# Two more gates in a pair and one written order on all engines, in the gate stage of a hybrid decoder step

## The chip, the core and the metric

The kernel runs on one core of a Trainium2 chip. The metric is the device time of one execution in microseconds (us). TensorE is the matrix engine (PE in the profile, its weight loads PEld), VectorE is DVE, ScalarE is ACT, GpSimd is POOL, and SyncE is SP, which here only issues transfers.

## What is computed

One layer of a decoder, for 512 prompt tokens and 8 sample tokens (one each), together N = 520 columns, D_MODEL = 2048. Two token mixers read the same normed input `h`. The first is a matrix memory and doesn't matter here. The second is forgetting attention with 8 heads of 128. A sigmoid gate for each channel merges them:

```python
mq, mk, mv, mo, mi, mf, fq, fk, fv, ff, ga, gb = jnp.split(h @ w_in + b_in, SPLIT_POINTS, axis=-1)
...
y_f = fox_fn(q_f, k_f, v_f, lf_f)
merged = jax.nn.sigmoid(ga) * (y_m @ w_proj_a) + jax.nn.sigmoid(gb) * (y_f @ w_proj_b)
x = x + g1 * (merged @ w_out)
```

For the prompt, `fox_prompt` is causal attention with cumulated log forget values added to the scores. For the samples, `fox_sample` takes 256 past keys and values of each sample from two pages of 128 rows in a cache, through a page table. A feed-forward part follows. All is float32; the kernel writes each operand as a high and a low part in a format that TensorE takes at full rate and sums three products (high by high, high by low, low by high).

## The kernel before

**Gates.** The pre-activations of `gb` are 16 chunks of 128 channels, called gates. Each is a product of 2048 rows of weights by `h`. There are two ways to compute one. `dense` (line 197) takes a gate by itself: 16 blocks by three products by two column halves are 96 matmuls of 260 columns. Its weights come in two halves of 1024 columns, each loaded raw (`wraw`, line 158), cast on ScalarE to `wh` and subtracted on VectorE to `wl` (`wtwo`, lines 164 to 169). A `GatePair` computes two gates at once by a scheme of seven products instead of eight on sums of the operands (`Pair`, `run_pairs`): 7 by 8 by 3 are 168 matmuls of 260 columns, plus sums of weights on VectorE. Pairs read the forms `hX` of `h`, and they stand in the stage before, between 8 pairs for queries and keys and 4 for values. `NB2 = 4` gates of `gb` are in pairs; the twelve others go through `dense` in the loop at line 1826, the gate stage.

**The second mixer behind the gates.** The attention is cut into small functions that are run between the matmuls of the gate stage. `dense` calls `step()` after every six matmuls, which takes the next entry of the list `bg`; the loop has 12 by 16 = 192 such steps. A table `plan`, filled by `put(step, function)` from line 1767 on, says what each step runs. Head hh starts at step b = 1 + 22 hh: it is loaded 20 steps earlier (`f_load`, five transfers on SP), normed (`f_norm`), split in high and low parts (`f_split` on ScalarE, `f_split_low` on VectorE at b + 4), its scores follow at b + 8 to b + 12 (`f_scores` on TensorE, `f_max` on VectorE with an exponential on ScalarE, `f_scale`), the turns of the weights at b + 19 on (`f_turn`, `f_turn_low`), and the products with the values at b + 26 to b + 29 (`f_attend`, whose last one also copies the result `yf`).

**Pages.** For the samples, 16 page pairs of keys (8 samples by two halves of the heads) are fetched by `s_load` (one row of q on SP, two gathers of 256 KB on POOL) at step 6 + 7i, and `s_scores` (step 18 + 7i) multiplies and reduces both pages on VectorE. Then `s_bias`, `s_turn`, `s_max`, `s_scale`, `s_weights` and `s_places` make the softmax from step 126 on, 32 gathers of values (`s_gather`) go out four for each of eight `s_attend` (tile `sO`, every five steps from 137), whose results are turned (`s_heads`, tile `sOT`) and added (`s_add`).

**What sets the order.** The kernel is written for a framework that places instructions on each engine's queue by their priority and by when it believes their operands ready, and gives out buffers from pools (33 tiles of tag `s`, nine `p`, seven `raw`, three each of `wh` and `wl`, four PSUM banks `mm`, two accumulators `acc`). `Ordered` (line 53) pins an instruction behind the one traced before it on its engine. In the pairs T, V and S (TensorE, VectorE, ScalarE) are pinned; in the gate stage only those of VectorE that are written through `MV`. Weight loads, casts and subtractions of `dense` are under a high priority, so they are placed as early as tiles allow. After the gates, sixteen products with `w_pb` follow (tile `pb`, from line 2001 on), which read `yf`.

Of the kernel before, what the change touches and what calls it, by code (L numbers as in the profile page):

```python
# [18 lines left out]
P = 128  # L19
# [3 lines left out]
NS = 8  # L23
# [40 lines left out]
def tile_hybrid_step(ctx: ExitStack, tc: tile.TileContext, I, O):  # L64
    nc = tc.nc
    S, V, G, T = nc.scalar, nc.vector, nc.gpsimd, nc.tensor
# [1194 lines left out]
    NB2 = 4  # L1261
# [133 lines left out]
    def root_load():  # L1395
        root["v"] = v = pt("rv")
        nc.sync.dma_start(v[:, :65], dss.rearrange("e h n -> (e h n)").rearrange("(p c) -> p c", p=P))
# [12 lines left out]
    def rows_load():  # L1410
        root["x"], root["r"] = pt("xr"), pt("rb")
        for e in range(2):
            o = slice(e * 64, e * 64 + 64)
            nc.sync.dma_start(root["x"][:, o].rearrange("p (h n) -> p h n", h=FH),
                              dqk[e, :, :, SEQ:N].rearrange("h p n -> p h n"))
            nc.sync.dma_start(root["r"][:, o].rearrange("p (h n) -> p h n", h=FH),
                              drr[e, :, SEQ:N].partition_broadcast(P))
# [12 lines left out]
    def s_rows(e):  # L1430
# [4 lines left out]
        nc.sync.dma_start(dqf[e].rearrange("b (h d) -> (b h) d", h=4), qrow[:32, :P])  # L1435

    def s_load(i):
# [3 lines left out]
        nc.sync.dma_start(qb[:, :512], dqf[e, b].partition_broadcast(P))  # L1441
# [4 lines left out]

    MV = Ordered(tc, nc.vector)
# [10 lines left out]
    def f_load(H):  # L1458
        H.q, H.k, H.rq, H.rk, H.v = (st("fi") for _ in range(5))
        for t, src in ((H.q, dqk[0, H.i]), (H.rq, drr[0, H.i].partition_broadcast(P)), (H.k, dqk[1, H.i]),  # L1460
                       (H.rk, drr[1, H.i].partition_broadcast(P)), (H.v, dv[H.i])):
            nc.sync.dma_start(t[:, :N], src)

    def f_norm(H):
        for t, w, r in ((H.q, qwc, H.rq), (H.k, nkw, H.rk)):
            MV.scalar_tensor_tensor(t[:, :N], t[:, :N], w, r[:, :N], op0=ALU.mult, op1=ALU.mult)
# [80 lines left out]
    T, V, S = nc.tensor, nc.vector, nc.scalar  # L1547
# [9 lines left out]
    psb = mm_ps("sbias")  # L1557
    o0 = psb[:, 0:64].rearrange("p (b h) -> p b h", b=NS)
    o1 = psb[:, 64:128].rearrange("p (b h) -> p b h", b=NS)
    T.matmul(o0, ups[:, :P], lg4[:, 0], start=True, stop=False)  # L1560
    T.matmul(o0, ones, lg4[:, 1], start=False, stop=False)
    T.matmul(o0, ones[:FH, :], lfd, start=False, stop=True)
    T.matmul(o1, ups[:, :P], lg4[:, 1], start=True, stop=False)
    T.matmul(o1, ones[:FH, :], lfd, start=False, stop=True)
    sbias = mconst([P, NPG, NS, FH], "sbias", tag="m0")
    V.tensor_copy(sbias, psb[:, :128].rearrange("p (g b h) -> p g b h", g=NPG, b=NS))


    vS = mconst([P, FH, NS], "vS")
    nc.sync.dma_start(vS, dv[:, :, SEQ:N].rearrange("h p n -> p h n"))  # L1570
# [8 lines left out]
    def lows(parts, src, n):  # L1579
        hi, lo = parts  # L1580
        MV.tensor_tensor(lo[:, :n], src[:, :n], hi[:, :n].bitcast(F32), op=ALU.subtract)
# [37 lines left out]
    def f_max(H, i):  # L1619
# [4 lines left out]
        MV.tensor_tensor_reduce(s[:, :n], ps[:, :n], H.nf[:, :n], 1.0, -3e38, ALU.add, ALU.max, sm[:, 0:1])  # L1624
        MV.tensor_scalar(sm[:, 0:1], sm[:, 0:1], -1.0, None, op0=ALU.mult)
# [6 lines left out]
    def f_scale(H, i):  # L1632
        n = (i + 1) * P
        s, sm = H.p[i], H.sm.pop(i)
        MV.reciprocal(sm[:, 1:2], sm[:, 1:2])
        MV.tensor_scalar(s[:, :n], s[:, :n], sm[:, 1:2], None, op0=ALU.mult)

# [15 lines left out]
    def f_attend(H, j):  # L1653
# [7 lines left out]
        T.matmul(H.y[:, j * P:], H.last[:, :P], H.last[:, P:2 * P], start=False, stop=True)  # L1661
        yf.append(st("yf"))
# [7 lines left out]
    def s_scores(i):  # L1670
        e, b = divmod(i, NS)
        qb, kps = W.k.pop(i)
        for g, kp in enumerate(kps):
            MV.tensor_tensor(kp[:, :512], kp[:, :512], qb[:, :512], op=ALU.mult)
            MV.tensor_reduce(sc[:, g, b, e * 4:e * 4 + 4], kp[:, :512].rearrange("p (h d) -> p h d", h=4),
                            axis=AX.X, op=ALU.add)

    def s_bias():
        MV.tensor_tensor(sc, sc, sbias, op=ALU.add)
# [1003 lines left out]
```

## Time and profile before

| | us |
|---|---|
| median of 3 runs (lowest, highest) | 2866.63 (2866.43, 2868.93) |
| the profiled execution's own time | 2859.93 |
| its span, from first to last instruction | 2858.2 |
| TensorE busy | 2825.6 |
| VectorE busy | 2164.1 |
| ScalarE busy | 1358.4 |

All rows below are of the one profiled execution, with times counted from the start of its span. Busy time is the union of an engine's instructions; instructions follow each other closer than their durations say, since each overlaps the next, so the work of a queue is read from start to start. PEclk is the granted TensorE clock as a share of its full one. In a list of waits, "A <- B" is A standing idle until B ended; `wl <- ACT wh` is VectorE waiting for ScalarE's cast.

### The profile page before, as it was taken

What the parts mean: (1) busy time and instruction counts of PE and PEld (TensorE: products, weight loads), DVE (VectorE), ACT (ScalarE), POOL (GpSimd) and SP (SyncE); (2) the same over time, 40 slices, a digit from 0 to 9 for tenths busy, and PEclk for the clock granted to TensorE, in tenths of its full rate; (3) what the DMA queues carried; (4) which work ended last, traced back from release to release, by engine and by line L of the source; (5) the groups of instructions that cost most, each with busy time, mean ns of one, the idle gap of its engine ahead of it and who ended that gap; (6) DMA issues with size and microseconds to landing.
All of it is one profiled execution on the core that took longest, in us unless ns stands there. A gap on an engine that the chain in (4) does not pass through costs nothing.

```text
span 2858.2 us, 57616 instructions
## 1 busy us (share of the span) xinstructions
PE 2825.6 (99%) x23318; PEld 2712.2 (95%) x23318; DVE 2164.1 (76%) x3334; ACT 1358.4 (48%) x2131; POOL 387.0 (14%) x671
## 2 busy tenths in 40 slices
PE   8999999999999999999999999999999999999999
PEld 6888998999999999799999999999999999999999
DVE  5986765576677777578888877878788888788787
ACT  4335543455555443444555444444444445444543
POOL 0001111211100222402111111101010101100100
PEclk9999999999999999999999999999999999999999
DMA  9946658845555587676772344444343346755753
GB/s 341 313 143 204 223 178 271 292 168 182 192 180 178 188 272 230 200 238 206 220 245 90 131 147 130 148 139 154 127 147 117 129 138 193 203 158 166 189 161 104
DMA packets 226755, 531.44 MB, mean 186 GB/s; under 512 B 30304, under 2 KB 83024, under 8 KB 226488
## 3 DMA queue, kind: packets, MB, share of 16 engines
q1 hardware_dynamic: 187296, 426.89, 46.3%
q0 software_dynamic: 38752, 100.64, 11.5%
q8 instruction: 183, 3.00, 0.4%
q14 instruction: 84, 0.69, 0.1%
q10 hardware_dynamic: 440, 0.23, 0.0%
HBM read 451.28 MB, written 72.92 MB: 183 GB/s over the span
## 4 chain that ended last, share of the span: by engine, by line
PE 88%; DMA 4%; DVE 4%; ACT 2%; issue 2%; SPq 0%; POOL 0%; ACTq 0%; DVEq 0%; POOLq 0%
PE x L60 34%; PE y L60 17%; PE z L60 9%; PE gate L213 4%; PE pa L213 3%; PE pb L213 3%; PE fo L60 3%; DMA ar<-in_w_ada 2%; PE mo L213 2%; PE pre L60 2%; PE mv L213 2%; PE adp L60 1%; PE adp L409 1%; PE mq L213 1%; PE mk L213 1%
## 5 line engine op out<-in xcount | busy, mean ns | idle before, releaser
L60 DVE TENSOR_TENSOR wl<-raw,wh 128x1024 fp32r<-128x1024 f32 (+1 forms) x666 | 801.8, 1204 | 351.2 <-ACT wh L60 348.0
L60 ACT CAST wh<-raw 128x1024 fp32r<-128x1024 f32 (+1 forms) x666 | 689.2, 1036 | 756.2 <-DVE raw L60 387.6
L60 PE MATMUL x<-bf,wh 128*128 128x260 f32 x2624 | 476.5, 283 | 0.0
L60 DVE TENSOR_TENSOR raw<-raw,raw 128x1024 f32<-128x1024 f32 x339 | 413.7, 1220 | 5.8
L60 PEld LDWEIGHTS x<-bf,wh 128*128 128x128 f32 x2624 | 403.3, 188 | 0.0
L60 PE MATMUL x<-bf,wl 128*128 128x260 f32 x1312 | 369.2, 281 | 0.0
L60 PEld LDWEIGHTS x<-bf,wl 128*128 128x128 f32 x1312 | 247.1, 188 | 0.0
L60 PE MATMUL y<-bf,wh 128*128 128x260 f32 x1312 | 239.3, 283 | 0.0
L168 DVE TENSOR_TENSOR wl<-raw,wh 128x1024 fp32r<-128x1024 f32 x92 | 112.6, 1224 | 125.3 <-ACT wh L167 121.5
L60 PEld LDWEIGHTS y<-bf,wh 128*128 128x128 f32 x1312 | 201.3, 188 | 0.0
L60 PE MATMUL x<-ff,wh 128*128 128x260 f32 x1024 | 186.3, 283 | 0.0
L60 PE MATMUL x<-hf,wh 128*128 128x260 f32 x1008 | 185.4, 284 | 0.0
L60 PE MATMUL y<-bf,wl 128*128 128x260 f32 x656 | 185.0, 282 | 0.0
L167 ACT CAST wh<-raw 128x1024 fp32r<-128x1024 f32 x92 | 96.5, 1049 | 181.5 <-issue 43.0
L60 PEld LDWEIGHTS x<-hf,wh 128*128 128x128 f32 x1008 | 154.9, 188 | 13.4 <-DVE tt L60 6.7
L60 PEld LDWEIGHTS x<-ff,wh 128*128 128x128 f32 x1024 | 157.7, 188 | 0.0
L60 PE MATMUL x<-ff,wl 128*128 128x260 f32 x512 | 144.7, 283 | 0.0
L60 PE MATMUL x<-hf,wl 128*128 128x260 f32 x504 | 142.2, 282 | 0.0
L60 PE MATMUL fo<-fe,wh 128*128 128x260 f32 x768 | 125.3, 284 | 1.1 <-DVE fo L60 0.9
L60 PEld LDWEIGHTS y<-bf,wl 128*128 128x128 f32 x656 | 123.5, 188 | 0.0
L60 PE MATMUL z<-bf,wh 128*128 128x260 f32 x656 | 119.9, 284 | 0.0
L60 PEld LDWEIGHTS fo<-fe,wh 128*128 128x128 f32 x768 | 105.6, 188 | 2.6 <-DVE fo L60 2.1
(640 smaller groups left out, 7050.9 us busy)
## 6 DMA issues: line engine op xcount, KB each, us to landing
raw<-in_w_fi SPq DMA_DIRECT2D x176, 512.0 KB, 4.0
raw<-in_w_in SPq DMA_DIRECT2D x155, 512.0 KB, 5.2
ar<-in_w_ada SPq DMA_DIRECT2D x192, 256.0 KB, 6.2
raw<-in_w_ada SPq DMA_DIRECT2D x96, 512.0 KB, 4.5
raw<-in_w_fo SPq DMA_DIRECT2D x64, 512.0 KB, 4.3
raw<-in_w_out SPq DMA_DIRECT2D x32, 512.0 KB, 4.8
raw<-in_w_fo SPq DMA_DIRECT2D x32, 384.0 KB, 3.5
dff<-cc POOLq DMA_DIRECT2D x44, 260.0 KB, 4.4
```

Of the source, the lines that this page charges most:

```text
L60: return lambda *a, **k: self.tc.keep_in_program_order(getattr(self.eng, op)(*a, **k))
L167: S.copy(wh[:, :n], raw[:, :n])
L168: V.tensor_tensor(wl[:, :n], raw[:, :n], wh[:, :n].bitcast(F32), op=ALU.subtract)
L213: T.matmul(acc[:, z, :HN], a[:, o], b[:, z * HN:(z + 1) * HN], start=(k == 0 and i == 0), stop=(k == K - 1 and i == 2))
L409: ins = T.matmul(ps[32 * g:32 * g + 32, :], cs[:, k, :], w, start=first, stop=last, tile_position=(0, 32 * g))
```

## The change

- `NB2` is 6: two more gates of `gb` are computed in a pair, ten are left for the gate stage, which has 160 steps.
- The gate stage no longer calls `dense`. Its matmuls are written out, and weight halves are loaded (`gate_load`, four halves ahead) and split (`gate_split`, two halves ahead) at fixed steps, without high priority. The first four loads and two splits stand in the last pair.
- Everything in this stage is pinned in the written order on all five engines: T, V, S stay `Ordered`, G and Y (POOL and SP) become so. `MV` goes.
- A head starts every 18 steps instead of 22 and is loaded 18 steps ahead; its result is copied by `f_result` two steps after its last product. A page pair comes every 5.5 steps, its two pages three steps apart, the first nine steps after its load (both twelve steps after, before). The softmax of the pages starts at step 104 instead of 126, page outputs come every four steps from 115 instead of every five from 137, and the copy of an output is two steps behind it. The offsets of the page scores (five small matmuls and a copy) stand in steps 3 and 5 instead of ahead of the stage.
- A gate's result is copied in the second step of the next gate (`gate_out`).

```diff
@@ tile_hybrid_step
-    S, V, G, T = nc.scalar, nc.vector, nc.gpsimd, nc.tensor
+    S, V, G, T, Y = nc.scalar, nc.vector, nc.gpsimd, nc.tensor, nc.sync
...
-    NB2 = 4
+    NB2 = 6
...
-    MV = Ordered(tc, nc.vector)
...
     t0, tq = 7 * (len(units) - 2), 7 * (2 * FH)
+    halves = [(j, e) for j in range(NB2, KC) for e in range(2)]
+    gw = {}
+
+    def gate_load(n):
+        if n < len(halves):
+            j, e = halves[n]
+            gw[n] = raw_tile()
+            Y.dma_start(gw[n], I["w_in"][1 + 24 + 24 + KC + j][:, e * 1024:(e + 1) * 1024])
+
+    def gate_split(n):
+        if n < len(halves):
+            gw[n] = wtwo(gw[n])
...
-                  t0 + 11: lambda: (s_load(0), s_load(1)), t0 + 13: on(f_norm, heads[0])}
+                  t0 + 8: lambda: (gate_load(0), gate_load(1)),
+                  t0 + 10: lambda: (gate_load(2), gate_load(3)), t0 + 11: lambda: (s_load(0), s_load(1)),
+                  t0 + 12: on(gate_split, 0), t0 + 13: lambda: (gate_split(1), f_norm(heads[0]))}
...
     run_pairs(units, late_steps, 0)
     hX = units = t = None
-    T, V, S = nc.tensor, nc.vector, nc.scalar
+    G, Y = (Ordered(tc, e) for e in (G, Y))
...
+    def s_offsets():
...
+    def s_keep():
...
+    def f_result(H):
         yf.append(st("yf"))
         S.copy(yf[-1][:, :SEQ], H.y)
...
-    def s_scores(i):
+    def s_scores(i, g):
...
-        if g == 1:
-            W.ob = pt("ob")
-            S.copy(W.ob[:, :512], W.o)
+
+    def s_copy():
+        W.ob = pt("ob")
+        S.copy(W.ob[:, :512], W.o)
...
-    HP = 22
+    HP = 18
...
-            put(b - 20, f_load, H)
+            put(b - 18, f_load, H)
...
-        put(max(148 + 4 * hh, b + 31), y_split, hh)
-        put(max(148 + 4 * hh, b + 31) + 1, y_low, hh)
+        put(b + 31, f_result, H)
+        put(max(124 + 4 * hh, b + 31), y_split, hh)
+        put(max(124 + 4 * hh, b + 31) + 1, y_low, hh)
+    put(3, s_offsets)
+    put(5, s_keep)
     for i in range(16):
         if i > 1:
-            put(6 + 7 * i, s_load, i)
-        put(18 + 7 * i, s_scores, i)
-    put(126, s_bias)
-    put(127, s_turn)
...
+            put(5 + 11 * i // 2, s_load, i)
+        put(14 + 11 * i // 2, s_scores, i, 0)
+        put(17 + 11 * i // 2, s_scores, i, 1)
+    put(104, s_bias)
+    put(104 + 1, s_turn)
...
     for i in range(8):
-        put(126 + i, s_gather, i)
+        put(104 + i, s_gather, i)
     for n in range(8):
-        t = 137 + 5 * n
+        t = 115 + 4 * n
         put(t, s_attend, n)
         for i in range(n * 4 + 8, min(n * 4 + 12, 32)):
-            put(t + 1 + i % 4, s_gather, i)
+            put(t + 1 + i % 4 * 4 // 5, s_gather, i)
         if n % 2:
-            put(t + 7, s_heads, n // 2)
-            put(t + 8, s_add, n // 2)
+            put(t + 2, s_copy)
+            put(t + 6, s_heads, n // 2)
+            put(t + 6 + 2, s_add, n // 2)
     for hh in range(FH):
-        put(183 if hh < FH - 1 else 188, y_sample, hh)
+        put(152 if hh < FH - 1 else 159, y_sample, hh)
...
-    bg += [on(run, plan[i]) if i in plan else None for i in range(max(plan) + 1)]
...
-    for j in range(NB2, KC):
-        i = 1 + 24 + 24 + KC + j
-        acc = dense(I["w_in"][i], h, "gate")
         t = st("sgm")
-        S.activation(z2(t), acc, AF.Identity, bias=col(C_BIN + i - 1))
+        S.activation(z2(t), acc, AF.Identity, bias=col(C_BIN + 48 + KC + j))
         G.dma_start(dsg[j], t[:, :N])
-    t = None
-    flush()
+
+    done = None
+    for n, (j, e) in enumerate(halves):
+        if e == 0:
+            acc = acc_ps("gate")
+        wh, wl = gw.pop(n)
+        for k in range(8):
+            xh, xl = h[8 * e + k]
+            o = slice(k * P, (k + 1) * P)
+            for i, (a, b) in enumerate(((wh, xh), (wh, xl), (wl, xh))):
+                for z in range(2):
+                    T.matmul(acc[:, z, :HN], a[:, o], b[:, z * HN:(z + 1) * HN],
+                             start=(e == 0 and k == 0 and i == 0), stop=(e == 1 and k == 7 and i == 2))
+            if k == 1:
+                if done:
+                    done()
+                done = None
+            if k == 2:
+                gate_split(n + 2)
+            if k == 3:
+                gate_load(n + 4)
+            run(plan.pop(8 * n + k, ()))
+        if e == 1:
+            done = on(gate_out, j, acc[:, :, :HN])
+    done()
...
+    T, V, S, G, Y = nc.tensor, nc.vector, nc.scalar, nc.gpsimd, nc.sync
```

Each `MV.` of the functions named above becomes `V.`, and each `nc.sync.` among them becomes `Y.`.

## Rows read from the trace of the kernel before

**Rows 1.** The page's first part: span, and each engine's busy time and share.

```profile
span 2858.2 us, 57616 instructions
PE 2825.6 (99%) x23318; PEld 2712.2 (95%) x23318; DVE 2164.1 (76%) x3334; ACT 1358.4 (48%) x2131; POOL 387.0 (14%) x671
```

**Rows 2.** Busy time by stretches: a late pair, the gate stage, parts of it.

```profile
core 0: us, PE busy (x) PEld busy (x) DVE busy (x) ACT busy (x) POOL busy (x), PEclk, DMA share, GB/s
960.00:983.00 23.00, 23.00 (x195) 23.00 (x194) 17.90 (x21) 10.91 (x15) 2.14 (x4) 1.00 0.38 122
1004.00:1217.00 213.00, 206.95 (x1574) 186.89 (x1574) 147.30 (x353) 94.47 (x207) 74.63 (x84) 0.99 0.71 232
1024.00:1124.00 100.00, 98.67 (x778) 94.34 (x777) 79.75 (x170) 42.47 (x90) 29.86 (x34) 1.00 0.75 243
1149.00:1153.00 4.00, 2.91 (x14) 2.51 (x15) 2.19 (x9) 1.15 (x5) 3.08 (x4) 0.61 0.88 304
1164.00:1217.00 53.00, 53.00 (x393) 43.34 (x393) 27.71 (x87) 25.10 (x59) 21.87 (x23) 1.00 0.59 187
```

**Rows 3.** Who waited for whom in the gate stage, TensorE and its weight load.

```profile
PE sS L1686 <- DVE sc L60: 2.9, 1, 2.9
PE gate L213 <- ACT sgm L1830: 1.5, 1, 1.5
PE fS L1194 <- ACT yf L1663: 1.1, 1, 1.1
PE vtp L1594 <- DVE fpl L60: 0.2, 1, 0.2
...
PEld sO L1731 <- DMA vp<-in_cache_v,idx: 1.6, 2, 1.1
```

**Rows 4.** TensorE's timeline: start us, us, instruction; where two pairs and the stages begin.

```profile
962.74 0.29 PE L60 MATMUL x<-hh,wh 128*128 128x260 f32 x1
...
982.83 0.29 PE L60 MATMUL x<-hh,wh 128*128 128x260 f32 x1
...
1004.14 0.43 PE L1564 MATMUL sbias<-lfd,ones 8*128 8x64 f32 x2
1004.50 0.51 PE L213 MATMUL gate<-hh,wh 128*128 128x260 f32 x2
...
1216.80 0.40 PE L213 MATMUL pb<-yfh,wh 128*128 128x260 f32 x2
```

**Rows 5.** The chain that ended last, in order of time: the product with w_pb.

```profile
1216.96 92.07 PE pb L213 x768
```

**Rows 6.** VectorE's instruction groups from 1004 to 1217 us.

```profile
line engine op names shapes xcount | busy us, mean ns | idle before us <-releasers
L168 DVE TENSOR_TENSOR wl<-raw,wh 128x1024 fp32r<-128x1024 f32 x24 | 29.4, 1225 | 40.1 <-ACT wh L167 37.1 <-PE fS L1616 2.9
...
L60 DVE TENSOR_TENSOR yfl<-yf,yfh 128x512 fp32r<-128x512 f32 x8 | 5.5, 684 | 1.3 <-ACT yfh L1576 1.3
```

**Rows 7.** VectorE's timeline: a gate half's subtraction and one page pair.

```profile
1051.06 1.22 DVE L168 TENSOR_TENSOR wl<-raw,wh 128x1024 fp32r<-128x1024 f32 x1
1052.19 0.69 DVE L60 TENSOR_TENSOR kp<-kp,qb 128x512 f32<-128x512 f32 x1
1052.91 0.69 DVE L60 TENSOR_REDUCE sc<-kp 128x4 f32<-128x512 f32 x1
1053.52 0.68 DVE L60 TENSOR_TENSOR kp<-kp,qb 128x512 f32<-128x512 f32 x1
1054.23 0.69 DVE L60 TENSOR_REDUCE sc<-kp 128x4 f32<-128x512 f32 x1
1054.84 0.68 DVE L60 TENSOR_TENSOR fql<-fi,fqh 128x512 fp32r<-128x512 f32 x1
```

**Rows 8.** The gather line on POOL: ns min/median/max, and its landings.

```profile
L868 POOL DMA_INDIRECT kp<-in_cache_k,idx x32: 942/967/1857, 988.8 to 1124.4; - x32
L868 POOL DMA_INDIRECT vp<-in_cache_v,idx x32: 942/950/1817, 1132.8 to 1193.5; - x32
...
DMA to landing us min/median/max: 2.2/4.2/8.7
```

**Rows 9.** TensorE's instruction groups, 960 to 1220 us: page outputs and their turns.

```profile
L1731 PE MATMUL sO<-vp,pp 128*32 128x512 f32 x64 | 12.6, 605 | 0.1
...
L1740 PE MATMUL sOT<-ident,ob 128*128 128x128 f32 x16 | 2.5, 276 | 0.0
```

More of the change, by code (lines that the diff above doesn't have):

```diff
@@ L1556, in tile_hybrid_step @@
     lg4 = lfg.rearrange("p (b g) h -> p g b h", g=NPG)
[L1557 to L1564, printed above, removed]
-    sbias = mconst([P, NPG, NS, FH], "sbias", tag="m0")
-    V.tensor_copy(sbias, psb[:, :128].rearrange("p (g b h) -> p g b h", g=NPG, b=NS))
+    sbias = mconst([P, NPG, NS, FH], "sbias", tag="m0")
+    def s_offsets():
+        psb = mm_ps("sbias")
+        o0 = psb[:, 0:64].rearrange("p (b h) -> p b h", b=NS)
+        o1 = psb[:, 64:128].rearrange("p (b h) -> p b h", b=NS)
+        T.matmul(o0, ups[:, :P], lg4[:, 0], start=True, stop=False)
+        T.matmul(o0, ones, lg4[:, 1], start=False, stop=False)
+        T.matmul(o0, ones[:FH, :], lfd, start=False, stop=True)
+        T.matmul(o1, ups[:, :P], lg4[:, 1], start=True, stop=False)
+        T.matmul(o1, ones[:FH, :], lfd, start=False, stop=True)
+        W.ps = psb
+    def s_keep():
+        V.tensor_copy(sbias, W.ps[:, :128].rearrange("p (g b h) -> p g b h", g=NPG, b=NS))
+        W.ps = None
     vS = mconst([P, FH, NS], "vS")
-    nc.sync.dma_start(vS, dv[:, :, SEQ:N].rearrange("h p n -> p h n"))
+    Y.dma_start(vS, dv[:, :, SEQ:N].rearrange("h p n -> p h n"))
     yf = []
@@ L1668, in tile_hybrid_step @@
     yS = mconst([P, NS, FH], "yS")
-    def s_scores(i):
+    def s_scores(i, g):
         e, b = divmod(i, NS)
[L1672 to L1676, printed above, removed]
+        qb, kps = W.k[i]
+        kp = kps[g]
+        V.tensor_tensor(kp[:, :512], kp[:, :512], qb[:, :512], op=ALU.mult)
+        V.tensor_reduce(sc[:, g, b, e * 4:e * 4 + 4], kp[:, :512].rearrange("p (h d) -> p h d", h=4),
+                        axis=AX.X, op=ALU.add)
+        if g == NPG - 1:
+            del W.k[i]
     def s_bias():
-        MV.tensor_tensor(sc, sc, sbias, op=ALU.add)
+        V.tensor_tensor(sc, sc, sbias, op=ALU.add)
     def s_turn():
         pqk = pt("pqk")[:, :64]
-        MV.tensor_tensor(pqk.rearrange("p (b e h) -> p e b h", b=NS, e=2), qS, kS, op=ALU.mult)
+        V.tensor_tensor(pqk.rearrange("p (b e h) -> p e b h", b=NS, e=2), qS, kS, op=ALU.mult)
         W.ps = ps = mm_ps("sS")
@@ L1771, in tile_hybrid_step @@
         if hh:
-            put(b - 20, f_load, H)
+            put(b - 18, f_load, H)
             put(b, f_norm, H)
+        put(b + 1, f_forget, H)
         put(b + 2, f_split, H)
+        put(b + 3, f_values, H)
         put(b + 4, f_split_low, H)
         put(b + 5, f_values_low, H)
-        put(b + 1, f_forget, H)
-        put(b + 3, f_values, H)
         for s, i in ((8, 0), (9, 1), (11, 2), (12, 3)):
@@ L1815, in run @@
             f()
-    assert not bg
-    bg += [on(run, plan[i]) if i in plan else None for i in range(max(plan) + 1)]
-    H = None
-    mg = [None] * KC
     def fetch_gate(j):
```

53 lines of the change are left out of this document (29 added, 24 removed).

## The prediction

> **What bounds the kernel now.** I read the page's first part first: TensorE is busy for 99% of the span [rows 1], so a change is worth what it takes off TensorE, in matmuls or in waits. Then I cut out the stage that the diff rewrites. The first gate matmul after the pairs starts at 1004.50 us, the first one of the product with w_pb at 1216.80 [rows 4]: 212.3 us for twelve gates, 192 steps. There VectorE is busy 147.3 us, and from 1024 to 1124 us 79.75 of 100 [rows 2]: the second engine, with a fifth of its time free. The list of who waited for whom shows four stops of TensorE, 5.7 us together, the longest 2.9 for the page scores `sc`; its weight load also stopped twice for `vp` pages, which I count as 0.6 us of lost time [rows 3]. Behind the long stop the granted clock is 0.61 over 4 us: part of it at the lower of its two levels, 1.2 GHz in place of 2.4 [rows 2]. That is 4 x 0.39 = 1.6 us, of which some 0.4 fell into the stop itself, so 1.2. Together the stage loses 5.7 + 0.6 + 1.2 = 7.5 us.
>
> **Two gates into a pair.** A gate is 96 matmuls of 260 columns. Undisturbed they follow each other every 92.07/768 = 0.120 us [rows 5], so two gates are 23.0 us. A pair makes both in 168 matmuls; from the start of the first product of one late pair to that of the next are 982.83 - 962.74 = 20.1 us [rows 4], with TensorE busy throughout and VectorE 17.9 of 23 us [rows 2], so the extra sums and splits of that pair lie beside its matmuls; were that cover gone, its sums would cost a few us. Its four raw loads and four stores meet DMA engines at a share of 0.38 [rows 2] and cost nothing on the path. Gain: **2.9 us**. Two sigmoids on the loaded gates go from the next stage to ScalarE in the pair, off the path both times.
>
> **Moves at no cost.** The offsets of the page scores are the same five small matmuls three steps later (two of them take 0.43 us [rows 4], all five some 0.6). Gate weights now load 15 steps (over 15 us) before their cast and are cast 14 steps before use; the longest landing of any gather beside them is 8.7 us [rows 8], and each half's cast plus subtraction is under 3 us. SP issues what it did, two gates less, but in written order: behind a head's five loads stand the q row of a page and a weight half. They wait only for free tiles, and those suffice up to step 109. POOL has the same gathers and stores in written order. A head's result is copied two steps later, so its PSUM bank is held longer; counting banks by step I find at most four at a time, which there are. Cover for all of this is the 9 to 15 steps of lead.
>
> **The shorter stage.** 160 steps instead of 192 carry the same attention. What TensorE does for it: 212.3 - 12 x 11.5 - 7.5 = 66.7 us, of which some 16 are the page outputs and their turns [rows 9] with some small neighbours; a head takes 50.7/8 = 6.3. VectorE: a half's subtraction takes 1.13 us of its queue, a page pair 2.65 (start to start) [rows 7]. So of 147.3 us, 24 halves are 27.1 and 16 pairs 42.4; of the rest, 77.8, about 8 belong to the late outputs (5.5 for `yfl` alone [rows 6]), and a head takes 69.8/8 = 8.7. Now one period of a head while pages come too:
> Before, 22 steps: TensorE 22 x 6 x 0.120 + 6.3 = 22.1 us; VectorE 8.7 + 2.75 x 1.13 + 3.14 x 2.65 = 20.1.
> After, 18 steps: TensorE 13.0 + 6.3 = 19.3; VectorE 8.7 + 2.25 x 1.13 + 3.27 x 2.65 = 19.9.
> So for about five periods (steps 14 to 104) **VectorE becomes the longer of the two** by 0.6 us a period, 3 us in all, even if it never idles. TensorE can be ahead of it: with b for a head's first step, the low parts of its queries and keys are written at b+4 and used at b+9, five steps or 5.3 us later, less the 1.2 us they take and some latency; I let 3.5 us be absorbed once. The new waiting time is then 5 x (19.9/(1 - i) - 19.3) - 3.5, where i is VectorE's idle share: nothing for i = 0, 4.7 us for 5%, 13 for 12%, 18.5 for 16%. Its bounds are 0 and, at the 20% of rows 2, about 24. Before, the largest part of VectorE's idle time was 37.1 us in front of gate halves, waiting for ScalarE's casts [rows 6], which the scheduler had put far ahead of the rest; now each half stands where it was written, with a cast of about 1 us just before it, and VectorE's backlog of page work mostly covers that. Two halves and a quarter in a period, half a us each, are 1.1 of 19.9: I take 5%, nearer the lower end for that reason, **4.7 us**.
>
> The other stops: the last page now stands five steps ahead of the bias and not three; of the 2.9 us I keep 1.0 (bounds 0 and 2.9). The stops for the copy of a gate and of a result should go: a gate is copied in the second step of the next one, 14 steps before its bank is needed. `vp` pages: four gathers in four steps where there were five; POOL starts one every 1.3 us at best (0.95 us each and its issue [rows 8]), 5.2 of the 5.9 us that four steps with a page output take, so they arrive just in time; 1.0 us (bounds 0 and the rival below). With the waits of about 1 us each I expect no lowered clock.
>
> **Sum.** -2.9 (pair) - 7.5 (waits and clock of before) + 4.7 + 1.0 + 1.0 = -3.7 us. The profiled execution took 2859.93 us (span 2858.2 and 1.7 around it), so 2856.2; the median of the three runs, 2866.63, is 6.7 above that execution, and carried over the forecast is **2862.9 us**. Differences under 0.2%, 5.7 us, a measurement of this kernel hardly tells from none; the forecast lies within.
>
> **The rivals.**
> *VectorE's excess stays hidden* (idle share about 1%): waits of 1.5 us in all: -2.9 - 7.5 + 1.5 = -8.9, **2857.7 us**. For it: everything VectorE needs is written one to two steps ahead of it, and a backlogged engine does not idle. Against: 79.75% in rows 2 is what a far looser schedule reached. Faster by over 0.2% needs an idle share under about 3%.
> *Slower: VectorE idles as it used to, and TensorE, pinned, can no longer go round it.* Place: steps 14 to 104, where each head's scores wait for its low parts. At 16% the price is 18.5 us: -2.9 - 7.5 + 18.5 + 2 = +10.1, **2876.7 us**. It decides for slower above an idle share of about 8%, by over 0.2% above 13%. For it: 20% idle in rows 2, and that scores, casts and sums now share one strict order, so that one late page holds them all. Against: the largest idle group of before has its cause removed.
> *The order cannot be held as written for lack of tiles.* I count 36 live tiles in steps 112 to 115 in the pool of 33 (five loads of the last head, eight split parts of two heads, four `vp` pages): ScalarE's copy of the last value block then stands until the first page output frees four, about 4 us. What is queued behind it (a gate's copy, a cast used 14 steps later) has cover; if not, 4 us: 2866.9.
> *The page gathers stretch.* Rows first: a gather took 967 ns in the median for keys, while VectorE was busy 80%, and 950 for values, while it was busy 27.7 of 53 us, with one at 1857 [rows 2, 8]. Were every value gather that long, four of them would take 7.4 us and more against 5.9 of TensorE, 1.7 us for each of seven outputs: +12, 2875. The Trainium skill, SBUF — State Buffer, section "SBUF: two separate sides", says that VectorE and GpSimd lock a shared port pair for a whole instruction, so that GpSimd can't write its descriptors meanwhile; by that rule this rival would win as VectorE fills up. The 2% between the two medians speak against it here.
>
> **How the numbers follow.** Forecast (idle share 3 to 13%, own range 2861 to 2872): 0.38, nearly all of it within 0.2%. Hidden excess: 0.33. Slower VectorE: 0.19. Too few tiles: 0.07, mostly within. Gathers: 0.03. So faster by over 0.2% 0.35, within 0.42, slower 0.23. The range reaches from a little below the second case to the third: 2855.5 to 2877, leaving out some 6% below and 12% above.
>
> **What would show it.** From the pairs' end to the first matmul of w_pb I expect 212.3 - 23.0 (two gates) - 0.8 (6.7 us of waits in place of 7.5) + 0.6 (the offsets, now inside) = 189.1 us, and one pair of 20.1 us more in front. VectorE's share between steps 14 and 104 should be about 95% instead of 80; stops of TensorE there should name `fkl`/`fql`, `fs` or a PSUM bank freed by VectorE; the stop before `sS` should be about 1 us, and no lowered clock behind it. Wrong would be: VectorE under 85% there with TensorE waiting for it (third case), TensorE without any stop there (second case), stops of several us in front of `sO` (gathers), or a gate matmul that waits for `wl` or a raw load, which I rule out.

## The result, and the profile after

The changed kernel took 2870.34 us (median of 22 runs, 2867.44 to 2873.64) beside 2866.36 us for the kernel before (22 runs, 2864.3 to 2868.93): a ratio of 1.0016, 95% interval 1.001 to 1.0022. That is 4.0 us more where 3.7 less were forecast: inside the range of the forecast, and inside the 0.2% that it called no change, but on the other side.

The page's first part, of the changed kernel (time 2870.03 us), beside [rows 1]:

```profile
span 2868.3 us, 57594 instructions
PE 2823.3 (98%) x23294; PEld 2712.1 (95%) x23294; DVE 2173.6 (76%) x3344; ACT 1360.6 (47%) x2137; POOL 389.6 (14%) x673
```

TensorE's timeline of the changed kernel, beside [rows 4], and the product with w_pb in its chain of waits, beside [rows 5]:

```profile
1023.98 0.40 PE L60 MATMUL gate<-hh,wh 128*128 128x260 f32 x2
...
1227.19 0.40 PE L213 MATMUL pb<-yfh,wh 128*128 128x260 f32 x2
```

```profile
1227.35 91.97 PE pb L213 x768
```

The first gate matmul starts 19.5 us later than before: that is the one pair more, forecast at 20.1, less the offsets of the page scores, which now stand behind it (0.6). From the first w_pb matmul to the end the two kernels agree within 0.3 us. So all of the rest lies in the gate stage: 203.2 us, where 189.1 were forecast and the twelve gates of before took 212.3.

Busy time by stretches, of the changed kernel, beside [rows 2]: the gate stage, steps 14 to 104, and step 104 to its end (a step is six gate matmuls; step 14 starts with the 85th).

```profile
core 0: us, PE busy (x) PEld busy (x) DVE busy (x) ACT busy (x) POOL busy (x), PEclk, DMA share, GB/s
1023.98:1227.19 203.21, 184.77 (x1389) 166.06 (x1387) 143.73 (x352) 88.51 (x201) 75.27 (x84) 0.97 0.70 230
1040.00:1144.00 104.00, 97.25 (x747) 92.03 (x746) 95.95 (x209) 45.74 (x105) 37.84 (x42) 0.98 0.76 243
1144.00:1227.19 83.19, 72.59 (x530) 60.15 (x529) 39.84 (x122) 33.86 (x81) 31.46 (x34) 0.96 0.59 199
```

Who waited for whom in the gate stage of the changed kernel (us in total, times, longest us), beside [rows 3]:

```profile
ACT fs L60 <- DVE sm L60: 53.1, 19, 7.9
...
POOL out_kT L60 <- DVE fi L60: 25.1, 5, 7.7
DVE wl L60 <- ACT wh L60: 20.0, 10, 4.4
...
PE fPT L60 <- DVE fs L60: 5.8, 5, 1.6
...
PE sO L60 <- issue: 4.0, 1, 4.0
...
PE vtp L60 <- ACT ob L60: 1.5, 1, 1.5
...
PE sO L60 <- DVE fpl L60: 1.4, 1, 1.4
PE sS L60 <- DVE sm L60: 1.4, 1, 1.4
...
PE sbias L60 <- POOL ups L60: 1.1, 1, 1.1
```

The old stops of TensorE, for a copy of a gate and of a result, are gone and the one before `sS` fell from 2.9 to 1.4 us. In their place stand new ones: the turn of a head's rows (`fPT`) waits for VectorE's scaling, page outputs (`sO`) and a head's values (`vtp`) for data or a PSUM bank. VectorE is 92% busy in steps 14 to 104 (95.95 of 104.00). In the whole stage it still waits 20 us for ScalarE's casts, and ScalarE 53 us for VectorE's maxima. The granted clock is 0.98 and 0.96 in the two stretches: part of each at 1.2 GHz in place of 2.4, behind such stops, which costs at most some 104 x 0.02 + 83 x 0.04 = 5.4 us (what fell into a stop cost nothing). The forecast had none.

The largest stop is odd. VectorE's and TensorE's timeline of the changed kernel near step 119:

```profile
1166.45 0.35 DVE L60 TENSOR_SCALAR fs<-fs,sm 128x256 f32<-128x256 f32 x1
...
1168.46 0.23 PE L60 MATMUL fS<-mask_f,identb 128*128 128x128 bf16 x1
...
1171.31 0.52 PE L60 MATMUL gate<-hh,wl 128*128 128x260 f32 x2
1175.16 0.56 DVE L60 CUSTOM_DVE_ANT_0 fs<-fS,nfb 128x384 f32<-128x384 f32 x1 [8.36 <-remote]
...
1175.78 0.98 PE L60 MATMUL sO<-vp,pp 128*32 128x512 f32 x4 [3.96 <-issue]
```

VectorE stands 8.4 us before a head's maximum, although the scores that it needs are recorded as finished at 1168.7; TensorE runs on for 3 us and then stands as well.

### The profile page after: what moved, and what is told of

Same layout as the page of the kernel before. It is cut to its first block, busy times and chain, and to the rows that moved or that the text cites. A ratio compares the mean times of both kernels' runs of the same rounds, so it can differ in the third digit from the quotient of the medians.

```text
span 2868.3 us, 57594 instructions
## 1 busy us (share of the span) xinstructions
PE 2823.3 (98%) x23294; PEld 2712.1 (95%) x23294; DVE 2173.6 (76%) x3344; ACT 1360.6 (47%) x2137; POOL 389.6 (14%) x673
## 4 chain that ended last, share of the span: by engine, by line
PE 55%; DVE 2%; ACT 1%; issue 1%; another core or an unknown queue 0%; POOL 0%; ACTq 0%; DVEq 0%; POOLq 0%
PE x L60 25%; PE y L60 13%; PE z L60 6%; PE fo L60 4%; PE pb L213 3%; PE gate L60 1%; ACT wh L60 1%; PE fg L60 1%; DVE wl L60 1%; PE adp L60 1%; DVE xa L60 0%; PE fa L60 0%; PE sO L60 0%; PE fy L60 0%
## 5 line engine op out<-in xcount | busy, mean ns | idle before, releaser
L60 DVE TENSOR_TENSOR wl<-raw,wh 128x1024 fp32r<-128x1024 f32 (+1 forms) x693 | 834.9, 1205 | 376.4 <-ACT wh L60 371.2
L60 ACT CAST wh<-raw 128x1024 fp32r<-128x1024 f32 (+1 forms) x693 | 717.5, 1036 | 766.3 <-DVE raw L60 391.1
L60 DVE TENSOR_TENSOR raw<-raw,raw 128x1024 f32<-128x1024 f32 x343 | 418.5, 1220 | 5.9
L60 PE MATMUL x<-hf,wh 128*128 128x260 f32 x1056 | 194.2, 284 | 0.0
L60 PEld LDWEIGHTS x<-hf,wh 128*128 128x128 f32 x1056 | 162.3, 188 | 13.4 <-DVE tt L60 6.7
L60 PE MATMUL x<-hf,wl 128*128 128x260 f32 x528 | 148.9, 282 | 0.0
L168 DVE TENSOR_TENSOR wl<-raw,wh 128x1024 fp32r<-128x1024 f32 x68 | 83.0, 1222 | 85.9 <-ACT wh L167 85.2
L167 ACT CAST wh<-raw 128x1024 fp32r<-128x1024 f32 x68 | 71.2, 1047 | 126.9 <-DMA raw<-in_w_in 41.2
```

The lines of the kernel that those rows point to most:

```text
L60: return lambda *a, **k: self.tc.keep_in_program_order(getattr(self.eng, op)(*a, **k))
L167: S.copy(wh[:, :n], raw[:, :n])
L168: V.tensor_tensor(wl[:, :n], raw[:, :n], wh[:, :n].bitcast(F32), op=ALU.subtract)
```

## The experiments

Four theories. **1:** VectorE's lateness sets the pace (its work, or its idle time in front of `wl`), and the pinned TensorE waits for it. **2:** POOL's written order, with stores that wait for other engines ahead of gathers, delays pages. **3:** tiles and banks tie the engines together. **4:** the 8 us stretch belongs to one execution. The runs fell on several chips, on which the kernel before took 2865.5 to 2866.9 us (A, B, F, G) or 2861.8 to 2862.0 (C, D, E); A is the result's own. All results, with the stage and its two stretches from the profiles:

| run | chip | ratio to before (95%) | gate stage us | steps 14-104 | step 104 to end |
|---|---|---|---|---|---|
| changed kernel | A | 1.0016 (1.001-1.0022) | 203.2 | 104.0 | 83.2 |
| after_again | B | 1.0008 (0.9999-1.0017) | 205.2 | 104.1 | 83.6 |
| after_third | F | 1.0014 (1.0005-1.0024) | 204.9 | 104.2 | 83.1 |
| after_same_chip | E | 0.9993 (0.9983-1.0002) | 193.4 | 104.1 | 73.3 |
| plain_values | G | 0.9979 (0.997-0.9989) | 195.0 | 104.1 | 73.3 |
| pool_free | C | 1.0002 (0.9993-1.0011) | 194.8 | 104.2 | 76.0 |
| pool_free_again | F | 1.0013 (1.0003-1.0022) | 205.5 | 104.2 | 86.7 |
| wl_later | C | 0.9972 (0.9961-0.9982) | 186.3 | 99.0 | 69.7 |
| wl_later_again | F | 0.9981 (0.9971-0.999) | 196.6 | 99.0 | 80.1 |
| exp_later | D | 0.9988 (0.9979-0.9997) | 191.8 | 100.2 | 75.7 |
| scale_act | C | 0.9993 (0.9984-1.0002) | 189.0 | 100.7 | 72.3 |
| no_page_product | B | 0.9955 (0.9941-0.9969) | 190.3 | 94.9 | 78.0 |
| all_three | C | 0.9941 (0.9928-0.9955) | 178.1 | 95.6 | 67.9 |
| all_three_again | F | 0.9976 (0.9965-0.9987) | 193.9 | 95.7 | 83.6 |
| order_alone (192 steps) | B | 0.9999 (0.999-1.0008) | 220.5 | | |
| gates_alone | B | 0.9995 (0.9986-1.0004) | 198.5 | | |
| order_wl_later (192) | D | 0.9973 (0.9961-0.9984) | 205.4 | | |
| all_three_four_gates (192) | D | 0.9953 (0.994-0.9967) | 203.6 | | |
| before_again (192) | E | 1.0002 (0.9992-1.0013) | 213.9 | | |

**The halves of the change.** First the written order with four gates in pairs and the old spacing:

```diff
-    NB2 = 6
+    NB2 = 4
-    HP = 18
+    HP = 22
-            put(5 + 11 * i // 2, s_load, i)
+            put(6 + 7 * i, s_load, i)
...
```

> The written order on all five engines (with the offsets, the copies and the page products as the change places them), but four gates in pairs, twelve behind them, and the old spacing: heads every 22 steps, pages every 7. Theory 1 (VectorE is the longer engine at 18 steps, and TensorE pinned must wait for it): at 22 steps VectorE has 20.1 us of work a period against 22.1 us of TensorE, so the waits are small: the gate stage, 212.3 us before, falls to about 206 (the 7.5 us of stops go, 1 or 2 stay), and the time is 2860 to 2863 us where the kernel before has 2866.4. Theory 2 (the written order by itself costs, because POOL's gathers stand behind stores that wait for VectorE and ScalarE, at any spacing): stops of TensorE in front of sO and sbias of 5 us and more as in the changed kernel, the stage 210 us or longer, time 2866 to 2870.

Then, as an edit of the kernel before, six gates in pairs and the new spacing, with only VectorE's attention work pinned:

```diff
-    NB2 = 4
+    NB2 = 6
-    HP = 22
+    HP = 18
...
```

> Six gates in pairs and ten behind them, heads every 18 steps and pages every 5.5, with TensorE, ScalarE, POOL and SP unpinned in the gate stage as before. Theory 1 with pinning as the harm (an unpinned TensorE goes round a late VectorE): the pair's 2.9 us are gained and few new stops come, 2861 to 2865 us. Theory 1 with VectorE's load as the harm whatever the order: VectorE's work of the stage does not fit and is left over at its end, the stage is 198 us or longer, 2867 to 2873 us. Theory 2: without the written order on POOL no stop in front of sO, 2861 to 2865 us.

Neither gained: 0.9999 and 0.9995. On the same chip the changed kernel took 2869.19 us and gates_alone 2865.59: with the new spacing, the rest of the written order (the other engines pinned, gates split at fixed steps) cost about 3.6 us there, though the intervals just overlap. With the written order alone the stage takes 220.5 us beside 212.3 of before, and TensorE's stops in front of `sS`, `fPT` and `sbias` are there as in the changed kernel. Who waited for whom, of order_alone:

```profile
PE sS L60 <- DVE sc L60: 4.5, 1, 4.5
PE fPT L60 <- DVE fs L60: 2.6, 3, 1.4
PE sbias L60 <- POOL ups L60: 2.4, 1, 2.4
```

So theory 1, in which 22 steps leave VectorE time enough, fell in that form; its order had to matter as well as its load. (The two stages are from different chips, so the 8 us are no measure of the order.)

**VectorE's load.** The first run leaves out the products of key pages with query rows; the second moves four scalings of a head to ScalarE.

```diff
-        V.tensor_tensor(kp[:, :512], kp[:, :512], qb[:, :512], op=ALU.mult)
         V.tensor_reduce(sc[:, g, b, e * 4:e * 4 + 4], ...
```

> The changed kernel without the product of each key page with its query row (32 instructions of VectorE of 0.68 us; the sums are made of the bare pages), so that VectorE has 17.7 us of work in 18 steps where TensorE has 19.3. Theory 1: the stops of TensorE in front of fPT, behind fs, and the lowered clock behind them go; the stage is some 8 us shorter, 2861 to 2864 us. Theory 2 (POOL's order): stops in front of sO stay as they are and those at fPT are not what costs; at most 2 us, 2868 to 2870 us. Theory 3 (tiles and banks tie the engines together): the same, at most 2 us.

```diff
-        V.tensor_scalar(s[:, :n], s[:, :n], sm[:, 1:2], None, op0=ALU.mult)
+    def f_times(H, i):
+        S.activation(s[:, :n], s[:, :n], AF.Identity, scale=sm[:, 1:2])
...
             put(b + s + 3, f_scale, H, i)
+            put(b + s + 5, f_times, H, i)
```

> The changed kernel with the four products that scale a head's rows (0.31, 0.37, 0.44 and 0.49 us, 1.6 us a head) on ScalarE, two steps after the reciprocal, in place of VectorE: VectorE's work is 18.3 us in 18 steps where TensorE has 19.3. Theory 1: the stops in front of fPT go to under 2 us, the lowered clock with them, 5 to 9 us less than the changed kernel, 2860 to 2864 us. Theory 2: sO unchanged, and at most 2 us less. Theory 3 (engines tied together through ScalarE's order): ScalarE's longer order makes it no faster, 2868 to 2872 us.

Busy time of no_page_product in steps 14 to 104:

```profile
1042.50:1137.40 94.90, 94.67 (x747) 90.56 (x747) 76.02 (x183) 46.67 (x107) 38.38 (x42) 1.00 0.78 257
```

With 20 us less work on VectorE the same steps take 94.9 us, TensorE is busy throughout and at full clock; on its chip the whole time falls by 0.5% of before against the changed kernel. VectorE's lateness is the cause there, and 94.9 is what the stretch costs without it. scale_act went the same way in the profile (104 to 100.7 us); its times fall into two groups (six of eleven at 2857, four at 2861.5 to 2863.3), so its ratio decides nothing.

**The idle time in front of `wl`.** A gate half is cast on ScalarE and at once subtracted on VectorE. The cast queues behind exponentials that wait for VectorE's own backlog of maxima. Two ways to break this ring: the subtraction four steps later, or the exponentials two steps later.

```diff
-                gate_split(n + 2)
+                gate_cast(n + 2)
             if k == 3:
                 gate_load(n + 4)
+            if k == 6:
+                gate_low(n + 2)
```

> The changed kernel with a gate half's subtraction on VectorE four steps after its cast on ScalarE instead of directly behind it. Theory 1 in the form that VectorE's idle time in front of wl (20 to 26 us in the stage, waiting for ScalarE, which itself waits for VectorE's maxima) is what makes it late: that idle time falls under 8 us, the stops in front of fPT fall from 5.8 to under 2 us, and the time by 4 to 6 us, to 2863 to 2865 us. Theory 1 in the form that only VectorE's work counts: the idle time moves to other places, the stops in front of fPT stay at 4 us or more, at most 2 us less. Theory 2: no change beyond 1 us.

```diff
-        S.activation(s[:, :n], s[:, :n], AF.Exp, bias=sm[:, 0:1], accum_out=sm[:, 1:2])
...
-            put(b + s + 3, f_scale, H, i)
+            put(b + s + 3, f_exp, H, i)
+            put(b + s + 4, f_scale, H, i)
```

> The changed kernel with each exponential of a head two steps later in ScalarE's order (the scaling behind it one step later), the gate half's subtraction again directly behind its cast. If VectorE stands in front of wl because the cast is queued on ScalarE behind an exponential that waits for VectorE's own backlog: that idle time falls from 20 to under 12 us, the stage from 203 to 205 to below 197 us, the time by 4 us or more, to 0.9970 to 1.0000 of the kernel before. If VectorE merely waits out the cast's own 1.05 us (18 halves, 19 us): the idle time stays at 17 us or more and the time within 2 us of the changed kernel, 1.0005 to 1.002 of the kernel before.

VectorE's group of these subtractions in steps 14 to 104 (count | busy us, mean ns | idle us before them), beside [rows 6]: of the changed kernel,

```profile
L60 DVE TENSOR_TENSOR wl<-raw,wh 128x1024 fp32r<-128x1024 f32 x11 | 13.4, 1219 | 5.0 <-ACT wh L60 5.0
```

of exp_later,

```profile
L60 DVE TENSOR_TENSOR wl<-raw,wh 128x1024 fp32r<-128x1024 f32 x11 | 13.4, 1219 | 1.8 <-ACT wh L60 1.8
```

and of wl_later, with its busy time in the two stretches:

```profile
L60 DVE TENSOR_TENSOR wl<-raw,wh 128x1024 fp32r<-128x1024 f32 x12 | 14.6, 1218 | 0.0
```

```profile
1043.00:1142.00 99.00, 96.34 (x748) 90.39 (x747) 95.89 (x209) 46.13 (x106) 38.16 (x41) 1.00 0.78 253
1142.00:1211.73 69.73, 67.75 (x529) 57.71 (x528) 40.31 (x123) 33.45 (x79) 31.93 (x34) 1.00 0.71 241
```

The five us of waiting vanish, the stretch falls by five us, and VectorE is 97% busy: it now does the same work with hardly a gap. The late stretch is shorter too, and the clock full in both. exp_later removes most of the wait in this stretch without touching the cast, so it was the queue on ScalarE and not the cast's own 1.05 us; but in the whole stage its idle time fell only from 20.0 to 17.7 us (8.3 of it in one late place), not under 12 as expected, and its ratio says nothing certain against 0.9993.

The same edit on the written order with the old spacing, and again beside the changed kernel on one chip:

> The written order alone at the old spacing (four gates in pairs, heads every 22 steps), with a gate half's subtraction four steps after its cast. If the subtraction directly behind its cast is what took the gain of the written order there too: VectorE's idle time in front of wl (24 us in the gate stage of the written order alone) nearly goes, the stage falls from 220.5 to 206 to 212 us, the time to 0.9960 to 0.9980 of the kernel before. If that matters only where VectorE is the longer engine (18 steps): the time stays at 0.999 or above.

> A gate half's subtraction four steps behind its cast, beside the changed kernel on the same chip. If VectorE's idle time in front of wl is the main loss: 5 to 8 us (0.17 to 0.28%) under the changed kernel on a chip without the stretch of standing engines, 10 to 13 us under it on a chip with it.

0.9973 at 22 steps, against 0.9999: the ring of waits took the gain of the written order there too. How much of that difference it took isn't shown, since B and D are chips of the two kinds; steps 14 to 104, which for the changed kernel take the same time on either kind, fall from 92.3 to 88.3 us. At 18 steps the edit gives 0.9972, no more: what two gates in a pair gain is about what VectorE's work takes back. On chip F it is 0.33% under the changed kernel (0.9981 and 1.0014).

**POOL's order.** A head's key store goes six steps behind its norm, a gate's store from the second to the sixth step of the next gate, and the triangle is built ahead of the pinned stretch:

```diff
-        G.dma_start(O["kT"][:, H.i, :], H.k[:, :N])
+    def f_store(H):
+        G.dma_start(O["kT"][:, H.i, :], H.k[:, :N])
...
-    G, Y = (Ordered(tc, e) for e in (G, Y))
...
+    G, Y = (Ordered(tc, e) for e in (G, Y))
     lfd = mconst([FH, NS, FH], "lfd")
...
+        put(b + 6, f_store, H)
...
-        G.dma_start(dsg[j], t[:, :N])
+        return lambda: G.dma_start(dsg[j], t[:, :N])
...
+            if k == 5:
+                if done:
+                    done()
```

> The changed kernel with POOL's written order freed of its waits: each head's key store stands six steps after its norm, a gate's store four steps after its copy, and the triangle for the offsets is built ahead of the pinned stretch. Theory 2 (stores ahead of gathers in POOL's order make value pages late): the stops of TensorE in front of sO (5.3 us) and of sbias (1.1 us) and the 8 us stretch in which VectorE stands before a head's maximum near 1170 us go, with the lowered clock behind them: 5 to 8 us less than the changed kernel, about 2862 to 2864 us. Theory 1 (VectorE's load): the stops in front of fPT (5.8 us) stay, sO loses only what sits behind POOL; at most 2 us less, 2867 to 2869 us.

> POOL's stores moved behind their waits, beside the changed kernel on the same chip. If POOL's order costs time on any chip: 0.1% or more under the changed kernel beside it. If it matters only where the stretch of standing engines appears: the same as the changed kernel within 0.1% on a chip without it, and 0.1 to 0.3% under it on a chip with it.

Of TensorE's stops of over 1 us that the changed kernel has on E, only the one before `sbias` goes (1.1 us): 1.0002 on C and 1.0013 beside 1.0014 on F. Theory 2 falls, although POOL's list of waits is long; its gathers have lead enough.

**Three edits together**, scale_act, wl_later and pool_free, with six and with four gates in pairs:

> The three edits of the runs beside it together. Theory 1 and theory 2 both true: their gains add up to about 10 us less than the changed kernel, 2857 to 2860 us, faster than both kernels, TensorE's stops in the stage under 6 us and the stage 190 to 193 us. If only one is true: as the better of the single edits, 2861 to 2865 us.

> The three edits together, beside the changed kernel on the same chip: 0.9941 of the kernel before, as before, on any chip; 15 us or more under the changed kernel.

> The three edits that gave 0.9941, on the written order with four gates in pairs and the old spacing. If two gates are worth 2.9 us where no stop is in the way: 2.9 us more than with six gates, 0.9951 of the kernel before, within the 0.0010 or so that such a measurement tells. If the tighter spacing still costs something: the same time as with six gates or less, 0.9941 or below.

Busy time in the two stretches of all_three, and all of TensorE's stops in its gate stage:

```profile
1037.60:1133.20 95.60, 94.65 (x746) 90.60 (x745) 90.14 (x196) 55.68 (x127) 39.42 (x42) 1.00 0.81 266
1133.20:1201.13 67.93, 67.60 (x529) 57.77 (x529) 34.92 (x105) 38.17 (x91) 31.75 (x34) 1.00 0.73 244
```

```profile
PE fPT L60 <- ACT fs L60: 0.8, 1, 0.8
PE sO L60 <- ACT ob L60: 0.3, 1, 0.3
```

This version beats both kernels on either kind of chip, 0.9941 and 0.9976 (medians 17.6 us less on C, 7.0 on F). On F 0.9941 was expected again: the late stretch takes 83.6 us there, no less than without the edits. With stops out of the way the two gates are worth 0.9953 less 0.9941, 3.4 us (2.9 forecast), but the two intervals overlap, so this size isn't shown.

No run tests theory 3 by itself. The stops for a bank, in front of `vtp` and `sO`, go in all_three, whose edits leave the number of banks as it is; that fits banks that only pass on the lateness of other engines.

**The chips.** The changed kernel was profiled three times more, and the kernel before once:

> The changed kernel, unaltered, for a second profile. Theory 4 (the stretch of 8.4 us near 1167 us in which all engines stand belongs to that one execution): no such stretch this time, the gate stage 195 to 198 us in place of 203.2, TensorE's other stops (fPT behind fs, some 6 us in all; sbias behind ups 1.1; sS 1.4; sOT 0.8) again there within 1 us. If it belongs to the kernel: the stretch again at the same instruction, and the stage 203 us. Time in both cases 2870 us.

> The kernel before, unaltered, for a second profile. If the profiled execution that the forecast was summed against was a lucky one (2859.93 us, under all 22 timed executions beside the changed kernel): this one's gate stage is 214 to 219 us in place of 212.3, with more lowered clock or longer stops in front of sS. If it was a chip that is faster everywhere: the stage is within 1 us of 212.3 and the difference lies ahead of the stage or behind it.

> The changed kernel on the same chip as the second profile of the kernel before. If the first profile of before was lucky: the gate stage of this one is longer than before's by less than the 10.1 us net that the first pair of profiles shows (one pair of 20.1 us, stage 9.1 shorter), net 3 to 6 us as the medians. If not: net 9 to 11 us.

> The changed kernel once more, as the measure for the three runs beside it on the same chip. If the sign of the change goes by the chip: 0.9985 to 1.0000 of the kernel before where that one takes about 2862 us, with no stretch near step 119 in which all engines stand, and 1.0005 to 1.002 where that one takes 2865 us or more, with such a stretch.

Theory 4 falls: the stretch was there again on B and F (8.1 and 8.4 us before the same maximum), and not on E. Busy time of after_same_chip in its two stretches:

```profile
1038.20:1142.30 104.10, 97.31 (x748) 92.05 (x747) 96.00 (x209) 45.63 (x105) 37.88 (x42) 0.98 0.76 242
1142.30:1215.59 73.29, 68.25 (x529) 57.62 (x529) 39.94 (x122) 33.97 (x81) 32.94 (x34) 1.00 0.69 227
```

and TensorE's stops of over 1 us in its steps after 104:

```profile
PE vtp L60 <- ACT ob L60: 1.5, 1, 1.5
PE sO L60 <- DVE fpl L60: 1.4, 1, 1.4
PE sS L60 <- DVE sm L60: 1.2, 1, 1.2
```

Steps 14 to 104 repeat within 0.2 us on all chips; the rest of the stage takes 73.3 us on E and 83.1 to 83.6 on A, B and F. On A and F the change is slower, on B probably (1.0008, from 0.9999); on E it is 0.9993, medians 2859.38 and 2861.82, though the interval reaches 1.0002. The profile of before that the forecast was summed against (2859.93 us, stage 212.3) is like the second one, on E (stage 213.9), and not like the timed runs of 2866.

The last run asked whether the gathers of value pages are behind it:

```diff
-        gather(W.v[i][:, :512], I["cache_v"], idx_h[e][:, b * NPG + g:b * NPG + g + 1])
+        G.dma_start(W.v[i][:, :512], I["cache_v"][i * P:(i + 1) * P, :])
```

> The changed kernel with its 32 gathers of value pages replaced by plain loads of as many fixed rows, issued from the same place of POOL's order (so the page outputs are made of other rows). Only on a chip where the kernel before takes 2865 us or more does it tell: there, if the gathers cause the stretch in steps 115 to 145 in which the engines stand, steps 104 to 160 take 73 to 75 us as on the faster chips and the time is 0.9985 to 1.0000 of the kernel before; if they do not, those steps take 83 us again and the time is 1.0008 to 1.0018. On a chip where the kernel before takes 2862 us: 0.999 to 1.000 either way.

It fell on a chip where the kernel before took 2866.3 us. Busy time in its two stretches, and VectorE before the same maximum:

```profile
1043.10:1147.20 104.10, 97.29 (x748) 92.06 (x747) 96.04 (x209) 45.90 (x105) 36.35 (x42) 0.98 0.78 245
1147.20:1220.48 73.28, 68.20 (x530) 57.58 (x530) 39.82 (x121) 33.97 (x81) 17.58 (x33) 1.00 0.66 223
```

```profile
1170.98 0.56 DVE L60 CUSTOM_DVE_ANT_0 fs<-fS,nfb 128x384 f32<-128x384 f32 x1 [1.93 <-PE fS L60]
```

73.3 us, the same as on E, and 0.9979. As many bytes from the same place in POOL's order, but without a list of rows: the 8.4 us became 1.9. On these chips the gathers cost the changed kernel some 10 us. That the gathers and not chip G make the difference rests on the time of the kernel before there, and on a second mark of these chips told in the last section; the changed kernel itself wasn't run on G.

## Why the prediction was wrong

*One pair more, 2.9 us:* nothing speaks against it. A late pair takes the 20.1 us forecast (980.92 to 1001.01 us, from start to start on A); what stands ahead of the stage grew by 19.5 us on A and 17.1 on E, so a profile tells this term no closer than that; two gates without stops gave 3.4 us by intervals that overlap.

*The stops of before go, 7.5 us:* right for the copies; `sS` kept 1.4 (1.0 forecast). The matmuls by themselves need less than reckoned: the stage of all_three without its stops is 177.0 us, against 189.1 - 6.7 = 182.4. These 5.4 us in the forecast's favour hid as much of what it had too small.

*VectorE becomes the longer engine:* right. It had 95.95 us of work in steps 14 to 104 where TensorE needs 94.65; the price with hardly any idle time is wl_later's 99.0 less 95.6 = 3.4 us; the forecast had 3 us and let TensorE's lead absorb it, and its formula gives 5 x (19.9/0.969 - 19.3) - 3.5 = 2.7 us for wl_later's idle share of 3.1%. **The idle share was mis-sized:** 5% was taken because VectorE's backlog would cover the casts; it was 1 - 95.95/104.0 = 7.7%. The forecast's own formula gives 5 x (19.9/0.923 - 19.3) - 3.5 = 7.8 us for that; measured are 104.0 - 95.6 = 8.4 in place of 4.7. What the step overlooked is that the cover turns against itself: ScalarE, which must cast, waits for the maxima that the backlog delays. The edges were seen one by one and not as a ring.

*Steps after 104, 2.0 us:* **this term failed most.** On A they cost 83.2 - 67.9 = 15.3 us. On E it is 73.3 - 67.9 = 5.4, most of it three stops: 1.2 us before `sS`, and 1.5 and 1.4 before `vtp` and `sO`, whose bank comes free only when ScalarE and VectorE, late by the same ring, have read it. The count of "at most four at a time" went by written steps, and the engines weren't at those steps. On A, B and F another 10 us come from the gathers. The rival with the gathers had them at 3%, and its sign came true (4.0 us in front of `sO`), but by another mechanism than the one it named: longer instructions on POOL. Those stayed as they were, beside [rows 8]; POOL's gathers of keys and of values in the changed kernel (ns min/median/max, first and last start):

```profile
L60 POOL DMA_INDIRECT kp<-in_cache_k,idx x28: 940/970/1769, 1034.9 to 1125.1; - x28
...
L60 POOL DMA_INDIRECT vp<-in_cache_v,idx x32: 942/946/1772, 1138.5 to 1201.4; - x32
```

Medians of 970 and 946 ns, where VectorE was 92% busy beside the first and 48% beside the second: no stretching with VectorE's load. The Trainium skill (SBUF — State Buffer, section "SBUF: two separate sides") describes the lock on the shared port pair for VectorE instructions in a two-port mode or with two SBUF inputs, a condition that the prediction left out; no lengthening by it shows in these medians.

*Too few tiles:* did not come. ScalarE's copy of the last value block in steps 112 to 115 starts without idle time (1158.00 us, behind the cast `fvh` at 1157.63).

*Offsets at no cost:* 1.1 us before `sbias`, since POOL builds their triangle late; pool_free shows it. *No lowered clock:* wrong, at most 5.4 us on A and 104 x 0.02 = 2.1 on E. *POOL's stores at no cost:* right.

*The sum:* all_three's stage of 178.1 us, with 8.4 more in steps 14 to 104, 15.3 after them and 1.3 ahead of them, is the 203.1 measured on A. **Carrying the difference from the one profile to the median, with a constant 6.7 us, was the step that lost the sign.** It took the change to be worth the same wherever the kernels run. Between before_again and after_same_chip, both on E, it came near: spans of 2861.0 and 2856.8 us, 4.2 less, and medians 2.4 apart, where 3.7 were forecast. That is in part luck: matmuls reckoned 5.4 us too long stood against waits reckoned 3.7 and 3.4 us too short. On the chips that gave the result the kernel before is 3.5 to 5 us longer than on C, D and E, the changed one 10 to 12 (2869.19 to 2871.18 against 2859.38). No row of the one profile could show that. The slower rival (VectorE idles, +10.1) had the right place and a share between its 5% and 16%, but not the size of the late part.

## What to carry to other kernels

Where every engine's order is written out, look for rings: a producer and its consumer on two engines should not stand next to each other when the producer's engine also waits for the consumer's; a few steps between them gave 0.2 to 0.3% here, more than the change itself moved. A bank or tile count by written steps is only as good as the lateness of the slowest engine. And before a profile's difference to the median is carried over as a constant, ask whether both come from the same chip.

## What had not been expected of the hardware

The same program stood some 10 us longer in one stretch on some chips than on others, to the same instruction, and plain loads in place of its indirect gathers ended that. TensorE's timeline of all_three_again, on F (its late stretch takes 83.6 us, on C 67.9):

```profile
1169.37 0.27 PE L60 MATMUL sOT<-ident,ob 128*128 128x128 f32 x1 [1.17 <-issue]
1171.53 0.27 PE L60 MATMUL sOT<-ident,ob 128*128 128x128 f32 x1 [1.89 <-issue]
1173.62 0.38 PE L60 MATMUL gate<-hh,wh 128*128 128x260 f32 x1 [1.82 <-issue]
1175.04 0.57 PE L60 MATMUL gate<-hh,wh 128*128 128x260 f32 x1 [1.04 <-issue]
```

Here turns and gate matmuls, whose operands were long there, go out one by one, with 1 to 2 us between them.

For VectorE's stand of 8.4 us the traces tell a little more. An engine signals the end of its work by raising a counter, a semaphore, and the traces hold these updates. On E every such update of TensorE, VectorE and ScalarE lies within 0.05 us of the recorded end of its instruction. On A TensorE's updates come late near step 119: taken in order, the one for the scores recorded as finished at 1168.69 us stands at 1175.14, and VectorE starts at 1175.16 (on F 1171.94, 1178.47 and 1178.50). So VectorE stood for TensorE's signal, not for a gather's data. The ends of matmuls are modelled, so whether the products or only their signals were late isn't shown. The gathers' data moved no slower: POOL's queue carried 2.36 MB in 11.1 us on A there, 1.84 MB in 8.9 us on E.

The two kinds of chip differ in their records too. The traces from A, B, F and G lack part of the semaphore updates (the changed kernel has 31001 on A, 31833 on E; 696 of the 832 that are missing belong to the gate stage), so that no landing of a transfer can be told in them; those from C, D and E, and the first one of the kernel before, tell 683 to 985. Steps 14 to 104 hold 1388 updates on A and 1728 on E, without a difference in time; the steps after them 761 and 1102. In plain_values they are 1420 and 1086: beside the gathers that were left updates are missing, as on A, and with the plain loads nearly all are there. That puts G with A, B and F. How the gathers bring this about, and whether the engines stood for them or for their being recorded, stays open: every timed run here has a recorded span and clock, so a cost of recording may be in the times. What the kernel before loses on the first kind (3.5 to 5 us) was not looked into.
